# HGRN2 scores of levels 1 to 16 and the diagonal as 32x32 blocks in four 32-column tiles, masked copies of 96 columns, and the streams' state products in small tiles

## The chip, the core and the metric

The kernel runs on one core of one Trainium2 chip. The metric is the device time of one execution in microseconds, as the median of several runs: 1744.59 us for the kernel before, median of 3 runs between 1742.51 and 1745.06. The five engines that matter are TensorE (PE, with its weight loads as PEld), VectorE (DVE), ScalarE (ACT), GpSimd (POOL) and SyncE (SP), which issues the DMAs.

## The reference

One layer with two head groups: stick-breaking attention and an HGRN2 recurrence, whose outputs are gated, projected and normalised. Inputs are one new stream of 2048 frames and eight running streams of 16 frames each. The change touches the HGRN2 part alone, of 4 heads with key and value size 128:

```python
def hgrn2_recurrence(q, k, g, i, s0):
    """S_t = diag(f_t) S_{t-1} + k_t outer i_t,  o_t = S_t^T q_t,  g = log f, k = 1 - f."""
    ...
    def step(S, xs):
        qc, kc, gc, ic = xs
        b = jnp.cumsum(gc, axis=2)
        diff = b[:, :, :, None, :] - b[:, :, None, :, :]
        decay = jnp.where(causal, jnp.exp(jnp.minimum(diff, 0.0)), 0.0)
        scores = jnp.einsum('bhtd,bhsd,bhtsd->bhts', qc, kc, decay)
        o = (jnp.einsum('bhts,bhsv->bhtv', scores, ic)
             + jnp.einsum('bhtd,bhdv->bhtv', qc * jnp.exp(b), S))
        b_last = b[:, :, -1:, :]
        S_new = (jnp.exp(b_last)[:, :, 0, :, None] * S
                 + jnp.einsum('bhsd,bhsv->bhdv', kc * jnp.exp(b_last - b), ic))
        return S_new, o
```

So within a chunk each pair of a key time s and a query time t >= s has a score, which is a dot product over 128 channels with a decay of its own for each channel.

## The kernel before

The program has two halves. The first multiplies the frames by `w_in` (groups `pj`, L313 to L315 and L323 to L325: three products for each block of the contraction, of a high and a low part of each operand) and stores or keeps the sections of the result. In the same half the HGRN2 part runs, as 24 **chains**: 4 heads times 6 tiles of time. A tile is 384 columns, that is three chunks of 128 frames; the last of each half of the frames differs: once its third chunk holds the eight running streams (4 chains, `smp`), and once there are only two chunks (4 chains). The second half does the attention (L742 to L811), the streams' attention and the output projection, and does not change.

A chain is a generator, `hgrn` (L405). `weave` calls it between groups of six to twelve projection matmuls, one step at a time; two chains that are open take turns. The order on each engine is thus the order in which Python emits the instructions: a step of a chain stands between two groups of `pj` matmuls, and every engine runs its own queue in order. PE waits in its queue if the operands of a chain's step are late.

Scores come by **levels** m = 1, 2, 4, ... 64. Time is halved again and again: at level m the pairs (s, t) count whose times lie in the two halves of one block of 2m frames. Before the product, `q` of the later half and `kS` (the keys, 1 - f) of the earlier half have been scaled by the decay up to the border between the halves (L455, L456; `tot` holds the decay of whole blocks, L459). For m below 32, `scores` (L427) makes the full 128x128 product of each chunk in fp32, into one PSUM tile `ps`, and a masked copy (`copy_predicated`, L447, 128x384) takes from it the pairs of this level into `sc`; the masks are `lev`. For m = 32 and 64 only the blocks that count are made (L443), in PSUM partitions that start at 0 or 64, and are copied (L450). A matmul in fp32 shows as two records in the trace, for its two passes.

The diagonal (s = t) goes another way: `dp` is the product of `q` and `kS` element by element (L423), split into a high part `dh` (ACT, L464) and a low part `dl` (POOL, L466), and a product with `ones` (L469, L470) sums it over the channels; a masked copy takes the diagonal (L471).

Then the keys are transposed (`pk`, `kN`), states are updated (`pu`, L486 to L497), and the output is `sc` times the values plus `q` times the states (`po`, L501 to L508). In an `smp` chain the third chunk has eight states `s0`, one for each stream. `qz` is `q` of the chunk spread over eight blocks of 128 columns, of which 16 are not zero (L479 to L481), and eight 128x128 products add up in one PSUM tile (L508). The new states come from two products of 512 columns (`pb`, L537) with `iz`, the values with all but one stream's rows zeroed (L532), followed by eight updates on DVE (L539).

PSUM tiles `ps` and `pb` come from a pool of two (`psc`). SBUF tiles of a chain (`hw`) have two buffers each.

Of the kernel before, what the change touches and what calls it, by code (L numbers as in the profile page):

```python
# [9 lines left out]
F32 = mybir.dt.float32  # L10
F32R = mybir.dt.float32r
U8 = mybir.dt.uint8
# [5 lines left out]
P = 128  # L18
# [30 lines left out]
def constants():  # L49
    i = np.arange(P)  # L50
    s, t = i[:, None], i[None, :]
    x = s ^ t
    lev = np.stack([(s < t) & (x >= m) & (x < 2 * m) for m in LEVELS[:NL]] + [s == t], 1)
    f = lambda a: np.ascontiguousarray(a, dtype=np.float32)
    c = {
        "ident": f(s == t),
        "ntri": f(np.where(t < s, 0.0, -2.0 ** 66)),
        "levels": f(lev),
        "tri16": f(np.arange(TS)[None, :] < (i % TS)[:, None]),
        "hmask": f((i // TS)[:, None] == np.arange(H)[None, :]),  # L60
    }
    return c
# [3 lines left out]
def stream_step_kernel(ctx: ExitStack, tc: tile.TileContext, x_prompt, x_sample, cache_k, cache_v, state_s,  # L66
# [19 lines left out]
    lev = cst.tile([P, NL + 1, P], U8, name="lev")  # L86
    hmask = cst.tile([P, H], F32, name="hmask")
# [19 lines left out]
    def copy(eng, dst, src):  # L107
        if eng is act:
            act.copy(dst, src)  # L109
        elif eng is pool:  # L110
            pool.tensor_scalar(dst, src, 1.0, None, ALU.mult)
        else:
            eng.tensor_copy(dst, src)
# [84 lines left out]
    with ExitStack() as ph:  # L198
# [206 lines left out]
        def hgrn(half, h, hg, t0, nch):  # L405
# [13 lines left out]
            dp = hw.tile([P, TW], F32, name="dp", tag="kN")[:, :n]  # L419
            dh = hw.tile([P, TW], F32R, name="dh", tag="dh")[:, :n]  # L420
            dl = hw.tile([P, TW], F32R, name="dl", tag="dl")[:, :n]
            pool.memset(sc[:, :nch], 0.0)
            dve.tensor_tensor(dp, q, kS, ALU.mult)  # L423
            dve.tensor_tensor(q, q, f, ALU.mult)
            yield

            def scores(k):  # L427
                ps = psc.tile([P, 4, P], F32, name="ps", tag="ps")
                for c in range(k):
                    mm(ps[:, c], ch(kS, c), ch(q, c), start=True, stop=True)  # L430
                return ps[:, :k]
# [3 lines left out]
            for li, m in enumerate(LEVELS):  # L435
                k = nch if m < TS else npr
                if m < BLK:
                    ps = scores(k)
                else:
                    ps = psc.tile([P, 4, P], F32, name="ps", tag="ps")  # L440
                    for s0_ in range(0, P, 2 * m):
                        for c in range(k):
                            mm(ps[s0_:s0_ + m, c, :m], kS[:, c * P + s0_:c * P + s0_ + m],  # L443
                               q[:, c * P + s0_ + m:c * P + s0_ + 2 * m], start=True, stop=True)
                def keep_scores():
                    if m < BLK:
                        dve.copy_predicated(sc[:, :k], lev[:, li:li + 1].to_broadcast([P, k, P]), ps)  # L447
                        return
                    for s0_ in range(0, P, 2 * m):
                        dve.tensor_copy(sc[s0_:s0_ + m, :k, s0_ + m:s0_ + 2 * m], ps[s0_:s0_ + m, :k, :m])  # L450
                nn = k * P
# [11 lines left out]
                if m == 2:  # L463
                    copy(act, dh, dp)  # L464
                if m == 4:
                    pool.tensor_tensor(dl, dp, f32(dh), ALU.subtract)  # L466
                yield
            ps = psc.tile([P, 4, P], F32, name="ps", tag="ps")[:, :nch]
            mm(ps, ones, dh, start=True, stop=False)  # L469
            mm(ps, ones, dl, start=False, stop=True)  # L470
            dve.copy_predicated(sc[:, :nch], lev[:, NL:NL + 1].to_broadcast([P, nch, P]), ps)  # L471
# [5 lines left out]
            if smp:  # L477
                qz = xr.tile([P, NB, P], F32, name="qz", tag="x")
                pool.memset(qz, 0.0)  # L479
                for b in range(NB):  # L480
                    pool.tensor_copy(qz[:, b, b * TS:(b + 1) * TS], ch(q, npr)[:, b * TS:(b + 1) * TS])  # L481
# [22 lines left out]
            if smp:  # L504
                c = npr
                mm(po[:, c], sc[:, c], iv(c), start=True, stop=False)
                for b in range(NB):
                    mm(po[:, c], qz[:, b], s0[:, b], start=False, stop=b == NB - 1)  # L508
# [20 lines left out]
            if smp:  # L529
                yield  # L530
                iz = qz
                pool.tensor_tensor(iz, iv(npr).unsqueeze(1).to_broadcast([P, NB, P]), bc(hmask, P), ALU.mult)  # L532
                yield
                for b in range(NB):
                    if b % 4 == 0:
                        pb = psc.tile([P, 4, P], F32, name="pb", tag="ps")
                        mm(pb, kN[:, npr], iz[:, b:b + 4], start=True, stop=True)  # L537
                    o = npr * P // TS + b
                    dve.scalar_tensor_tensor(s0[:, b], s0[:, b], tot16[:, o:o + 1], pb[:, b % 4], ALU.mult, ALU.add)  # L539
                defer(lambda: dma.dma_start(s_sample[0, :, h].rearrange("b d e -> d b e"), s0), 2)  # L540


        def small():
            levf = xr.tile([P, NB, P], F32, name="levf", tag="x")[:, :NL + 1]
# [757 lines left out]
```

## Time and profile before

The profiled execution took 1747.05 us, with a span of 1745.2 us from its first to its last instruction.

| engine | busy us | share of the span | instructions |
|---|---|---|---|
| PE | 1672.4 | 96% | 12901 |
| PEld (weight loads) | 1519.8 | 87% | 12901 |
| DVE | 971.0 | 56% | 1762 |
| ACT | 710.9 | 41% | 1641 |
| POOL | 776.6 | 44% | 870 |

A matmul's record begins when it starts to read its moving operand and ends when the modelled result is there, so records of consecutive matmuls overlap, and the cost of one in a stream is the distance from its start to the next one's start. Views of the trace that are used: the page (shares of engines, the span in 40 slices), the table of stages (busy time of each engine in a stretch of the span), the groups by line and shape (count, busy time, mean duration of one, idle time before and who ended it), the waits (who waited for whom), and the timeline, in which neighbours of one line and shape are merged: start, length from the first start to the last end, and count.

### The profile page before, as it was taken

How to read it: one execution, taken by the hardware profiler on the slowest of the kernel's cores; microseconds unless marked ns; L12 is line 12 of the kernel's file. 1: busy time of each engine (PE TensorE's matmuls, PEld its weight loads, DVE VectorE, ACT ScalarE, POOL GpSimd, SP SyncE). 2: the span in 40 equal slices, each digit the busy share in tenths (PEclk: the TensorE clock that was granted, in tenths of full speed). 3: DMA queues.
4: the chain of work that ended last, by engine and by line, in shares of the span. 5: the costliest groups of instructions: out<-in, count | busy, mean ns of one | idle time of the engine just before them, and what ended most of it. 6: DMA issues, size and time to landing. Idle time of an engine off the chain costs nothing.

```text
span 1745.2 us, 33561 instructions
## 1 busy us (share of the span) xinstructions
PE 1672.4 (96%) x12901; PEld 1519.8 (87%) x12901; DVE 971.0 (56%) x1762; ACT 710.9 (41%) x1641; POOL 776.6 (44%) x870
## 2 busy tenths in 40 slices
PE   8999999999989999999999978999999999999998
PEld 8999999999989999999999966877887777778886
DVE  4264444255634263641647337787887686665554
ACT  3231221221323132221223246777877897775110
POOL 1242313232341142221323346777777776665664
PEclk9999999999999999999999989999999999999999
DMA  4233132122345133231212388899795754431443
GB/s 156 62 108 105 61 98 81 41 72 67 94 129 166 37 110 87 67 111 43 73 51 90 111 208 168 195 206 237 166 222 123 216 160 113 100 89 60 133 146 115
DMA packets 298790, 204.12 MB, mean 117 GB/s; under 512 B 113532, under 2 KB 275848, under 8 KB 298632
## 3 DMA queue, kind: packets, MB, share of 16 engines
q1 hardware_dynamic: 298632, 201.98, 43.5%
q8 instruction: 103, 1.69, 0.4%
q14 instruction: 55, 0.45, 0.1%
HBM read 146.36 MB, written 56.10 MB: 116 GB/s over the span
## 4 chain that ended last, share of the span: by engine, by line
PE 81%; DVE 5%; ACT 4%; DMA 4%; issue 2%; POOL 2%; SPq 1%; POOLq 0%; DVEq 0%; ACTq 0%
PE pj L313 10%; PE pj L315 10%; PE pj L314 10%; PE po L795 6%; PE z L742 5%; PE wt L777 5%; PE ps L430 4%; PE pj L323 4%; PE pj L325 4%; PE pj L324 4%; PE py L1132 3%; PE py L1134 3%; PE py L1133 3%; PE pk L877 2%; DVE kS L456 2%
## 5 line engine op out<-in xcount | busy, mean ns | idle before, releaser
L313 PE MATMUL pj<-xh,wh 128*128 128x384 f32 (+1 forms) x1152 | 395.7, 343 | 0.0
L764 POOL TENSOR_TENSOR s<-s,pr 128x512 f32<-128x512 f32 (+3 forms) x320 | 324.1, 1019 | 120.0 <-DVE pr L711 97.9
L315 PE MATMUL pj<-xh,wl 128*128 128x384 f32 (+1 forms) x1152 | 376.2, 327 | 0.0
L314 PE MATMUL pj<-xl,wh 128*128 128x384 f32 (+1 forms) x1152 | 375.7, 326 | 0.0
L117 POOL TENSOR_TENSOR wl<-wr,wh 128x512 fp32r<-128x512 f32 x126 | 164.2, 1327 | 387.9 <-ACT wh L109 387.9
L711 DVE TENSOR_TENSOR_SCAN pr<-keep,pr,one 128x513 f32<-128x513 f32 x192 | 238.6, 1270 | 46.7 <-ACT keep L750 35.0
L313 PEld LDWEIGHTS pj<-xh,wh 128*128 128x128 f32 x1152 | 217.4, 189 | 3.0 <-issue 1.0
L314 PEld LDWEIGHTS pj<-xl,wh 128*128 128x128 f32 x1152 | 217.5, 189 | 0.7 <-issue 0.7
L315 PEld LDWEIGHTS pj<-xh,wl 128*128 128x128 f32 x1152 | 216.7, 188 | 0.0
L742 PE MATMUL z<-kst,qr 128*128 128x512 f32 (+3 forms) x640 | 187.6, 404 | 17.9 <-ACT keep L750 6.3
L109 ACT COPY wh<-wt 128x512 f32<-128x512 f32 (+3 forms) x320 | 165.9, 550 | 78.4 <-PE wt L777 76.7
L747 ACT ACTIVATE s<-z 128x512 f32<-128x512 f32 (+3 forms) x320 | 184.6, 577 | 16.3 <-PE z L744 9.7
L777 PE MATMUL wt<-ident,s 128*128 128x128 f32 x1088 | 165.0, 279 | 2.1 <-POOL s L764 1.9
L323 PE MATMUL pj<-wh,xh 128*128 128x256 f32 x544 | 161.2, 296 | 0.0
L324 PE MATMUL pj<-wl,xh 128*128 128x256 f32 x544 | 153.0, 281 | 0.8 <-POOL wl L117 0.8
L777 PEld LDWEIGHTS wt<-ident,s 128*128 128x128 f32 x1088 | 123.2, 142 | 34.9 <-issue 16.4
L325 PE MATMUL pj<-wh,xl 128*128 128x256 f32 x544 | 152.8, 281 | 0.0
L117 POOL TENSOR_TENSOR e<-ev,e 128x384 fp32r<-128x384 f32 (+1 forms) x48 | 45.3, 943 | 221.1 <-ACT e L109 152.4
L795 PEld LDWEIGHTS po<-wh,vst 128*64 128x64 f32 x2176 | 119.1, 138 | 26.4 <-issue 16.2
L742 PEld LDWEIGHTS z<-kst,qr 128*128 128x128 f32 x640 | 106.0, 197 | 39.7 <-ACT keep L750 19.9
L795 PE MATMUL po<-wh,vst 128*64 128x128 f32 x2176 | 138.5, 279 | 0.0
L750 ACT ACTIVATE keep<-z 128x512 f32<-128x512 f32 (+2 forms) x230 | 134.6, 585 | 0.0
(164 smaller groups left out, 2907.0 us busy)
## 6 DMA issues: line engine op xcount, KB each, us to landing
wr<-in_w_in SPq DMA_DIRECT2D x64, 512.0 KB
qr<-qT_d SPq DMA_DIRECT2D x64, 256.0 KB
kr<-in_cache_k SPq DMA_DIRECT2D x16, 1024.0 KB
vr<-in_cache_v SPq DMA_DIRECT2D x32, 512.0 KB
kst<-kT_d SPq DMA_DIRECT2D x24, 512.0 KB
mt<-mx_d SPq DMA_DIRECT2D x136, 64.0 KB
x<-in_x_prompt SPq DMA_DIRECT2D x16, 512.0 KB
out<-xr SPq DMA_DIRECT2D x16, 512.0 KB
```

What stands on the lines that cost most here:

```text
L117: eng_lo.tensor_tensor(lo, src, f32(hi), ALU.subtract)
L313: mm(o, wh[:, k], xh[:, k, :n], start=k == 0, stop=False)
L314: mm(o, wh[:, k], xl[:, k, :n], start=False, stop=False)
L315: mm(o, wl[:, k], xh[:, k, :n], start=False, stop=k == KT - 1)
L323: mm(o, xh[:, k, ts], wh[:, k], start=k == 0, stop=False)
L324: mm(o, xh[:, k, ts], wl[:, k], start=False, stop=False)
L325: mm(o, xl[:, k, ts], wh[:, k], start=False, stop=k == KT - 1)
L711: dve.tensor_tensor_scan(pr[:, CW - wd:CW + 1][:, ::-1], kr, by, carry, ALU.mult, ALU.bypass)
L742: mm(z[:, :wd], q[:, a, r, q0:q0 + P], k[:, a, k0:k0 + wd], start=r == 0, stop=r == 1 and not top)
L764: pool.tensor_tensor(s[:, :wd], s[:, :wd], pr[:, CW - wd + 1:CW + 1], ALU.mult)
L777: nc.tensor.transpose(pt_[:, x:x + P], U[(u, a)][0][:, x:x + P], ident)
L795: mm(o[r], v[:, lo // P % 8 + x, r], th[a][:, x * P:(x + 1) * P], start=top and x == 0, stop=bot and x == n - 1, skip_group_check=True)
```

## The change

1. The masks `lev` shrink from 128 to 32 columns for each level: column j of row s now stands for the time that lies j into the 32-block of s.
2. For m below 32, `near` makes four 32x32 products per chunk instead of one 128x128 product: those of the 32-blocks on the diagonal of the chunk. Block number i of a chunk is written to PSUM partitions 32i to 32i+31, which are the array's column tile i; the four follow each other, chunk by chunk.
3. The masked copies (`keep`) have 96 columns (three chunks of 32), into a new tile `sd`, which POOL clears. At level 32, four copies on POOL bring `sd` into the diagonal blocks of `sc`.
4. The diagonal (s = t) is made by `near` too, of `q0`, the unscaled `q`, into other columns of the PSUM bank that level 1 uses; `dp`, `dh`, `dl` and the products with `ones` are gone. So that `q0` stays, the scaled `q` has a tile of its own, `qf`.
5. At levels 32 and 64 the loops are swapped: chunk by chunk, and the column tiles within.
6. In `smp` chains, `qz` has 32 columns for each stream instead of 128. The eight products go into 32 output partitions each, that is into the column tile that holds the two streams of 16 frames; streams 0, 2, 4, 6 first and then 1, 3, 5, 7. `iz` has four blocks instead of eight; the two `pb` products contract over 64 partitions each (0 to 63 and 64 to 127) and follow each other before the eight DVE updates.

```diff
@@ -49,15 +49,16 @@
 def constants():
     i = np.arange(P)
     s, t = i[:, None], i[None, :]
-    x = s ^ t
-    lev = np.stack([(s < t) & (x >= m) & (x < 2 * m) for m in LEVELS[:NL]] + [s == t], 1)
+    u = s // BLK * BLK + np.arange(BLK)[None, :]
+    x = s ^ u
+    lev = np.stack([(s < u) & (x >= m) & (x < 2 * m) for m in LEVELS[:NL]] + [s == u], 1)
     f = lambda a: np.ascontiguousarray(a, dtype=np.float32)
     c = {
 ...
         "levels": f(lev),
         "tri16": f(np.arange(TS)[None, :] < (i % TS)[:, None]),
-        "hmask": f((i // TS)[:, None] == np.arange(H)[None, :]),
+        "hmask": f((i // TS % 4)[:, None] == np.arange(4)[None, :]),
     }
     return c
 
@@ -83,8 +84,8 @@
     ntri = cst.tile([P, P], F32R, name="ntri")
     ones = cst.tile([P, P], F32R, name="ones")
     pool.memset(f32(ones), 1.0)
-    lev = cst.tile([P, NL + 1, P], U8, name="lev")
-    hmask = cst.tile([P, H], F32, name="hmask")
+    lev = cst.tile([P, NL + 1, BLK], U8, name="lev")
+    hmask = cst.tile([P, 4], F32, name="hmask")
 
     qT_d = scr.tile([4, 2, P, T], F32, name="qT_d")
     kT_d = scr.tile([4, 2, P, T], F32, name="kT_d")
@@ -416,38 +417,49 @@
             kS = hw.tile([P, TW], F32, name="kS", tag="kS")[:, :n]
             dve.tensor_scalar(kS, f, -1.0, 1.0, ALU.mult, ALU.add)
             sc = hw.tile([P, 3, P], F32, name="sc", tag="sc")
-            dp = hw.tile([P, TW], F32, name="dp", tag="kN")[:, :n]
-            dh = hw.tile([P, TW], F32R, name="dh", tag="dh")[:, :n]
-            dl = hw.tile([P, TW], F32R, name="dl", tag="dl")[:, :n]
+            sd = hw.tile([P, 3, BLK], F32, name="sd", tag="sd")
+            q0, q = q, hw.tile([P, TW], F32, name="qf", tag="qf")[:, :n]
             pool.memset(sc[:, :nch], 0.0)
-            dve.tensor_tensor(dp, q, kS, ALU.mult)
-            dve.tensor_tensor(q, q, f, ALU.mult)
-            yield
-
-            def scores(k):
-                ps = psc.tile([P, 4, P], F32, name="ps", tag="ps")
+            pool.memset(sd[:, :nch], 0.0)
+            dve.tensor_tensor(q, q0, f, ALU.mult)
+            yield
+
+            def near(ps, q, k):
                 for c in range(k):
-                    mm(ps[:, c], ch(kS, c), ch(q, c), start=True, stop=True)
-                return ps[:, :k]
+                    for s0_ in range(0, P, BLK):
+                        r = slice(c * P + s0_, c * P + s0_ + BLK)
+                        mm(ps[s0_:s0_ + BLK, c], kS[:, r], q[:, r], start=True, stop=True)
+
+            def keep(ps, li, k):
+                dve.copy_predicated(sd[:, :k], lev[:, li:li + 1].to_broadcast([P, k, BLK]), ps[:, :k])
 
             tot = f
             tot16 = None
             for li, m in enumerate(LEVELS):
                 k = nch if m < TS else npr
+                bank = psc.tile([P, 4, P], F32, name="ps", tag="ps")
+                ps = bank[:, :, :BLK]
                 if m < BLK:
-                    ps = scores(k)
+                    if li == 0:
+                        p0 = bank[:, :, BLK:2 * BLK]
+                        near(p0, q0, nch)
+                    near(ps, q, k)
                 else:
-                    ps = psc.tile([P, 4, P], F32, name="ps", tag="ps")
-                    for s0_ in range(0, P, 2 * m):
-                        for c in range(k):
+                    ps = bank
+                    for c in range(k):
+                        for s0_ in range(0, P, 2 * m):
                             mm(ps[s0_:s0_ + m, c, :m], kS[:, c * P + s0_:c * P + s0_ + m],
                                q[:, c * P + s0_ + m:c * P + s0_ + 2 * m], start=True, stop=True)
+
                 def keep_scores():
                     if m < BLK:
-                        dve.copy_predicated(sc[:, :k], lev[:, li:li + 1].to_broadcast([P, k, P]), ps)
+                        if li == 0:
+                            keep(p0, NL, nch)
+                        keep(ps, li, k)
                         return
                     for s0_ in range(0, P, 2 * m):
                         dve.tensor_copy(sc[s0_:s0_ + m, :k, s0_ + m:s0_ + 2 * m], ps[s0_:s0_ + m, :k, :m])
+
                 nn = k * P
                 q4 = q[:, :nn].rearrange("p (b two m) -> p b two m", two=2, m=m)
                 k4 = kS[:, :nn].rearrange("p (b two m) -> p b two m", two=2, m=m)
@@ -460,15 +472,11 @@
                 tot = nt
                 if m == 8:
                     tot16 = nt
-                if m == 2:
-                    copy(act, dh, dp)
-                if m == 4:
-                    pool.tensor_tensor(dl, dp, f32(dh), ALU.subtract)
+                if m == BLK:
+                    for s0_ in range(0, P, BLK):
+                        r = slice(s0_, s0_ + BLK)
+                        pool.tensor_copy(sc[r, :nch, r], sd[r, :nch])
                 yield
-            ps = psc.tile([P, 4, P], F32, name="ps", tag="ps")[:, :nch]
-            mm(ps, ones, dh, start=True, stop=False)
-            mm(ps, ones, dl, start=False, stop=True)
-            dve.copy_predicated(sc[:, :nch], lev[:, NL:NL + 1].to_broadcast([P, nch, P]), ps)
             pk = pt.tile([P, 4, P], F32, name="pk", tag="pt")
             for c in range(nch):
                 nc.tensor.transpose(pk[:, c], ch(kS, c), ident)
@@ -476,9 +484,10 @@
             act.copy(kN[:, :nch], pk[:, :nch])
             if smp:
                 qz = xr.tile([P, NB, P], F32, name="qz", tag="x")
-                pool.memset(qz, 0.0)
-                for b in range(NB):
-                    pool.tensor_copy(qz[:, b, b * TS:(b + 1) * TS], ch(q, npr)[:, b * TS:(b + 1) * TS])
+                pool.memset(qz[:, :, :2 * TS], 0.0)
+                for a in range(2):
+                    pool.tensor_copy(qz[:, a::2, a * TS:(a + 1) * TS],
+                                     ch(q, npr).rearrange("p (b a t) -> p b a t", a=2, t=TS)[:, :, a])
             yield
             po = pho.tile([P, 4, P], F32, name="po", tag="po")
             pu = pt.tile([P, 4, P], F32, name="pu", tag="pt")
@@ -503,9 +512,10 @@
                     mm(po[:, c], ch(q, c), olds[c], start=False, stop=True)
             if smp:
                 c = npr
-                mm(po[:, c], sc[:, c], iv(c), start=True, stop=False)
-                for b in range(NB):
-                    mm(po[:, c], qz[:, b], s0[:, b], start=False, stop=b == NB - 1)
+                mm(po[:, c], sc[:, c], iv(c), start=True, stop=True)
+                for b in [*range(0, NB, 2), *range(1, NB, 2)]:
+                    r = slice(b // 2 * 2 * TS, (b // 2 + 1) * 2 * TS)
+                    mm(po[r, c], qz[:, b, :2 * TS], s0[:, b], start=False, stop=True, skip_group_check=True)
             ms = hw.tile([P, 4], F32, name="ms", tag="ms")
             mo = hw.tile([P, 3, P], F32, name="mo", tag="mo")
             for c in range(nch):
@@ -528,20 +538,23 @@
                 dma.dma_start(s_prompt[0, 0, h], st[h][(c0 // 3 + 3 * half + 1) % 3])
             if smp:
                 yield
-                iz = qz
-                pool.tensor_tensor(iz, iv(npr).unsqueeze(1).to_broadcast([P, NB, P]), bc(hmask, P), ALU.mult)
+                iz = qz[:, :4]
+                pool.tensor_tensor(iz, iv(npr).unsqueeze(1).to_broadcast([P, 4, P]), bc(hmask, P), ALU.mult)
                 yield
+                pbs = []
+                for b in range(2):
+                    pbs.append(psc.tile([P, 4, P], F32, name="pb", tag="ps"))
+                    r = slice(b * DH, (b + 1) * DH)
+                    mm(pbs[b], kN[r, npr], iz[r], start=True, stop=True)
                 for b in range(NB):
-                    if b % 4 == 0:
-                        pb = psc.tile([P, 4, P], F32, name="pb", tag="ps")
-                        mm(pb, kN[:, npr], iz[:, b:b + 4], start=True, stop=True)
+                    pb = pbs[b // 4]
                     o = npr * P // TS + b
                     dve.scalar_tensor_tensor(s0[:, b], s0[:, b], tot16[:, o:o + 1], pb[:, b % 4], ALU.mult, ALU.add)
                 defer(lambda: dma.dma_start(s_sample[0, :, h].rearrange("b d e -> d b e"), s0), 2)
 
 
         def small():
-            levf = xr.tile([P, NB, P], F32, name="levf", tag="x")[:, :NL + 1]
+            levf = xr.tile([P, NL + 1, BLK], F32, name="levf", tag="x")
             dma.dma_start(levf, levels_d)
             dma.dma_start(hmask, hmask_d)
             vraw = xr.tile([12, P], F32, name="vraw", tag="x")
```

Three places in the order of instructions. First PE at the start of a chain's scores. Before, three 128x128 products `ps` stand between two groups of the projection:

```order
L315 MATMUL pj<-xh,wl 128x384
L430 MATMUL ps<-hq,kS 128x128 x3
L313 MATMUL pj<-xh,wh 128x384
L314 MATMUL pj<-xl,wh 128x384
L315 MATMUL pj<-xh,wl 128x384
```

With the change the same place holds twelve products of the unscaled `q` (named `hq`) for the diagonal and twelve of level 1 (named `qf`); the next levels have twelve each:

```order
L316 MATMUL pj<-xh,wl 128x384
L431 MATMUL ps<-hq,kS 32x32 x12
L431 MATMUL ps<-qf,kS 32x32 x12
L314 MATMUL pj<-xh,wh 128x384
L315 MATMUL pj<-xl,wh 128x384
L316 MATMUL pj<-xh,wl 128x384
```

The products have become smaller and four times as many, and those of the diagonal have moved from the chain's end to its first step; the projection around them is unchanged.

Second PE at the output of an `smp` chain, where `st` and `stt` are the states of the new stream and `s` those of the running streams. Before:

```order
L501 MATMUL po<-hi,sc 128x128
L503 MATMUL po<-stt,hq 128x128
L506 MATMUL po<-hi,sc 128x128
L508 MATMUL po<-s_1482,qz 128x128 x8
L313 MATMUL pj<-xh,wh 128x384
```

and with the change:

```order
L510 MATMUL po<-hi,sc 128x128
L512 MATMUL po<-stt,qf 128x128
L515 MATMUL po<-hi,sc 128x128
L518 MATMUL po<-s_1592,qz 32x128 x8
L314 MATMUL pj<-xh,wh 128x384
```

The eight products keep their place and write 32 partitions each.

Third POOL in the first `smp` chain, where `wl` is the low part of the projection's weights and `rs` belongs to the norm of the output. Before:

```order
L117 TENSOR_TENSOR wl<-wr,wh 128x512 x2
L422 MEMSET sc 128x384
L466 TENSOR_TENSOR dl<-dp,dh 128x384
L479 MEMSET qz 128x1024
L481 COPY qz<-hq 128x16 x8
L131 TENSOR_SCALAR rs<-ms 128x3
L132 TENSOR_TENSOR rs<-rs,nhalf 128x3
L117 TENSOR_TENSOR wl<-wr,wh 128x512 x2
L532 TENSOR_TENSOR qz<-hi,hmask 128x1024
```

and with the change:

```order
L118 TENSOR_TENSOR wl<-wr,wh 128x512 x2
L422 MEMSET sc 128x384
L423 MEMSET sd 128x96
L478 COPY sc<-sd 32x3x32 x4
L487 MEMSET qz 128x8x32
L489 COPY qz<-qf 128x4x16 x2
L132 TENSOR_SCALAR rs<-ms 128x3
L133 TENSOR_TENSOR rs<-rs,nhalf 128x3
L118 TENSOR_TENSOR wl<-wr,wh 128x512 x2
L542 TENSOR_TENSOR qz<-hi,hmask 128x512
```

The subtraction for `dl` is gone and four copies have come in, three levels later; the clearing of `qz` covers a quarter of the columns, its eight copies have become two, and the product with `hmask` is half as wide.

## The prediction

> **What bounds the kernel now.** I read the table of stages first, then the waits of PE, then the timeline of PE around a chain's step. The stages (length, then busy time with instruction count of PE, PEld, DVE, ACT, POOL, the granted clock, DMA):
>
> ```profile
> 0.00:60.00 60.00, 53.63 (x373) 51.93 (x374) 22.75 (x49) 18.96 (x32) 10.12 (x15) 1.00 0.44 141
> 60.00:1008.00 948.00, 927.42 (x6626) 902.18 (x6624) 437.04 (x1094) 222.18 (x567) 273.13 (x308) 1.00 0.29 85
> 1008.00:1100.00 92.00, 74.01 (x589) 60.44 (x591) 56.94 (x69) 59.32 (x137) 55.56 (x78) 0.87 0.80 177
> 1100.00:1745.00 645.00, 617.33 (x5319) 505.28 (x5315) 454.25 (x550) 410.44 (x907) 437.78 (x470) 0.99 0.61 153
> ```
>
> From 60 to 1008 us, where projection and chains run, PE is busy 927 of 948 us at full clock, DVE 437, POOL 273, and the DMA engines at 0.29. So PE alone bounds this half, and a microsecond taken from PE's queue there is a microsecond of the kernel. The second half has no instruction of the change; I take it as shifted as a whole. What PE waits for in the first half (total, times, longest):
>
> ```profile
> PE ps L430 <- DVE kS L456: 8.4, 9, 1.4
> PE pq L522 <- DVE on L518: 2.6, 3, 1.3
> PE ps L430 <- DVE sc L447: 2.6, 2, 1.3
> PE pb L537 <- POOL qz L532: 2.5, 1, 2.5
> ...
> PE ps L469 <- DVE sc L450: 1.1, 2, 0.7
> PE ps L430 <- DVE tot L459: 1.1, 4, 0.3
> ```
>
> Some 18 us, of which 15.8 us for DVE's work in the chains: small, but not nothing.
>
> **What one block of scores costs PE now.** The timeline of PE (start, length to the last end, line, count):
>
> ```profile
> 85.96 0.34 PE L315 MATMUL pj<-xh,wl 128*128 128x384 f32 x1
> 86.14 0.83 PE L430 MATMUL ps<-hq,kS 128*128 128x128 f32 x6
> 86.72 0.42 PE L313 MATMUL pj<-xh,wh 128*128 128x384 f32 x1
> 86.98 0.34 PE L314 MATMUL pj<-xl,wh 128*128 128x384 f32 x1
> 87.16 0.34 PE L315 MATMUL pj<-xh,wl 128*128 128x384 f32 x1
> 87.33 0.33 PE L313 MATMUL pj<-xh,wh 128*128 128x384 f32 x1
> ```
>
> A projection matmul follows the other by 0.175 us (86.98 to 87.33 is two). From 85.96 to 86.98 are 1.02 us; less two such steps the block of three chunks costs 0.67 us, that is 0.111 us for each of its six records. Two chunks cost 0.45.
>
> **What a block of 32x32 products costs.** Level 32 does them already, in two column tiles, six products (12 records) one tile after the other:
>
> ```profile
> 940.18 0.34 PE L315 MATMUL pj<-xh,wl 128*128 128x384 f32 x1
> 940.44 0.47 PE L443 MATMUL ps<-hq,kS 128*32 128x32 f32 x12
> 940.84 0.44 PE L313 MATMUL pj<-xh,wh 128*128 128x384 f32 x1
> 941.12 0.34 PE L314 MATMUL pj<-xl,wh 128*128 128x384 f32 x1
> 978.66 0.33 PE L443 MATMUL ps<-hq,kS 128*32 128x32 f32 x8
> ```
>
> 940.18 to 941.12, less 0.35, is 0.59 us. A record here takes 0.20 us by itself (L443 below), so first to last start is 0.27 us and **0.32 us are lost to entering and leaving the small tiles**: the first starts 0.26 us after a projection matmul, and the projection's second start comes 0.28 us after its first. That price is paid once per block, whatever is in it. How fast four tiles run together is seen in the streams' attention of the second half, with records of 128 columns:
>
> ```profile
> 1102.04 0.43 PE L958 MATMUL so<-vs,swN 128*32 128x128 f32 x8
> 1102.28 1.93 PE L958 MATMUL so<-vr,swT 128*32 128x128 f32 x64
> 1102.03:1102.07 0.04, 0.03 (x4) 0.03 (x5) 1.00 0.71 154
> ```
>
> 64 records from first to last start take 1.93 - 0.27 = 1.66 us, 26 ns each: four tiles carry 128 columns every 0.105 us, each as fast as the whole array above. The last row counts four starts within 40 ns. For 32 columns one tile needs a quarter of 0.111, 28 ns, at least; the row x8 (four records in each of two tiles, 0.13 us from first to last start) allows 43 at most. I take 32, near the lower end, since the x8 row holds the slow first weight load. Three chunks give each tile six records: 0.05 + 4 x 0.032 + 0.02 for the stagger of the tiles = **0.20 us**, and the block 0.52. Two chunks give 0.14, the doubled blocks of level 1 0.40 (three chunks) and 0.27 (two).
>
> **The sum on PE.** Counts and prices by these groups (count | busy, mean ns | idle before):
>
> ```profile
> L430 PE MATMUL ps<-hq,kS 128*128 128x128 f32 x672 | 95.4, 276 | 12.0 <-DVE kS L456 8.4 <-DVE sc L447 2.6 <-DVE tot L459 1.1
> L443 PE MATMUL ps<-hq,kS 128*32 128x32 f32 x256 | 10.0, 200 | 0.2 <-DVE kS L456 0.2
> L447 DVE COPY_PREDICATED sc<-lev,ps 128x384 f32<-128x384 uint8 x96 | 56.3, 586 | 0.0
> L447 DVE COPY_PREDICATED sc<-lev,ps 128x256 f32<-128x256 uint8 x24 | 10.6, 443 | 0.0
> L469 PE MATMUL ps<-dh,ones 128*128 128x384 f32 x20 | 7.1, 354 | 1.1 <-DVE sc L450 1.1
> L469 PE MATMUL ps<-dh,ones 128*128 128x256 f32 x4 | 1.2, 303 | 0.0
> L537 PE MATMUL pb<-qz,kN 128*128 128x512 f32 x16 | 9.1, 700 | 2.5 <-POOL qz L532 2.5
> ```
>
> The masked copies count the blocks: 96 of three chunks and 24 of two; 20 and 4 of them are level 1.
> - Levels 2 to 16: 76 blocks x (0.52 - 0.67) = -11.4; 20 of two chunks x (0.46 - 0.45) = +0.2.
> - Level 1, with the diagonal's products: 20 x (0.72 - 0.67) = +1.0; 4 x (0.59 - 0.45) = +0.6.
> - Products with `ones` gone: 20 x 2 x 0.175 = -7.0; 4 x 2 x 0.12 (two thirds of it) = -1.0.
> - Level 32 in turns: 16 blocks of three chunks, 0.27 to 0.19 = -1.3; two chunks and level 64 unchanged.
> - Output of the running streams, now:
>
> ```profile
> 160.08 1.95 PE L508 MATMUL po<-s,qz 128*128 128x128 f32 x16
> ```
>
>   16 records at 0.111 = 1.78 us; then four rounds of four tiles at 0.11, plus 0.32 = 0.76. Four chains: -4.1.
> - New states: four records of 512 columns, each 0.43 (between 4 x 0.105 and 4 x 0.111), 1.71 us a chain. No row shows two tiles of 64 rows at once. Ends: one after the other, with the switch, 2.03 (+1.3 in all), or together, 0.86 + 0.32 = 1.18 (-2.1). I take together, since column tiles do run so (L958).
>
> Together **-25 us**.
>
> **What goes beside PE.** DVE: from 586 and 443 ns for 384 and 256 columns, 1.1 ns a column, a copy of 96 is an estimated 0.26 us; 120 of them save 0.3 each, the diagonal's product and copy another 1 us a chain. This is worth something only where PE waits for DVE: a level's three DVE operations shorten from 1.7 us (0.51 + 0.61 + 0.59, L455, L456, L447) by a fifth:
>
> ```profile
> L455 DVE TENSOR_TENSOR hq<-hq,tot 128x192 f32<-128x192 f32 x108 | 55.0, 509 | 36.7 <-PE ps L430 26.0 <-PE ps L443 10.2
> L456 DVE TENSOR_TENSOR kS<-kS,tot 128x192 f32<-128x192 f32 x108 | 65.7, 608 | 0.0
> L466 POOL TENSOR_TENSOR dl<-dp,dh 128x384 fp32r<-128x384 f32 x20 | 21.1, 1072 | 6.8 <-ACT dh L109 6.8
> L481 POOL COPY qz<-hq 128x16 f32<-128x16 f32 x32 | 4.7, 198 | 4.1 <-DVE hq L455 3.9
> L532 POOL TENSOR_TENSOR qz<-hi,hmask 128x1024 f32<-128x1024 f32 x4 | 7.6, 1899 | 0.0
> L117 POOL TENSOR_TENSOR wl<-wr,wh 128x512 fp32r<-128x512 f32 x126 | 164.2, 1327 | 387.9 <-ACT wh L109 387.9
> ```
>
> Bounds for those waits: none of 15.8 goes, or all; as PE's shorter blocks also leave DVE less time, I take a quarter, **-4**, and -1 of the 2.5 us for `qz`, whose product halves. POOL: `dl` goes (1.07 us a chain), four copies of 32x96 come, at 0.2 (a 128x16 copy) to 0.4 us: no net load. The first waits for DVE's last masked copy, and behind it in POOL's queue stand `wl` for the next section and the stores' low parts; POOL idles 388 us before `wl`, waiting for ACT, which is the cover. Without it each `wl` that is late would cost PE up to 1.3 us. The copies themselves are needed by `po` three steps later, several us. The new DVE wait, for the clearing of `sd`, stands right behind that for `sc`.
>
> **Total:** -25 - 5 = -30 us. The profiled execution took 1747.05 us and would take 1717; the median of the runs stands 2.5 us below it, so the forecast is **1715 us**.
>
> **The rivals.**
> 1. *Small records don't come that fast (slower).* L443's twelve records stand 0.27/11 = 24.5 ns apart on the mean. In a block of 24 the mean distance p has to be paid 23 times; over all blocks (76 x 23 + 20 x 15 + 20 x 47 + 4 x 31 = 3112 distances) the sum without waits is 3112 p - 52 us (my p, 0.20/23 = 8.7 ns, gives the -25 back). It turns at p = 16.8 ns. With 24.5 it is +24: **1769**. For it: no row shows more than a dozen such short records. Against it: x8 has 0.13/7 = 18.5 ns with two tiles, so tiles overlap, and four of them start within 40 ns in L958. Chance 0.11. The Trainium skill's "TensorE: Matmul & The Clock Gate", section "Wait — 56ns, not 53.3ns?", states that the distance of starts never falls below about 25 ns, however few columns; by that rule the sum would be an estimated +26 us, 1771. The count of four starts in 40 ns disagrees with it across tiles, though nothing here shows it for long.
> 2. *Queueing in between.* A near block has 48 loads and matmuls within 0.2 us, level 1 96; if they are supplied only every 13 ns a record, the sum is 3112 x 0.013 - 52 = -12: **1733**. The same comes if PE, faster now, waits for `kS` twice as long (+16 against -25 gives 1736). Chance 0.18.
> 3. *More goes:* all 18 us of waits with the 25: **1702**. Chance 0.09.
> 4. *Both halves of rival 2 together*, or a later start of the attention's loads (DMA 0.80 behind 1008 us): no change, 1741 to 1748. Chance 0.07.
>
> **How the numbers follow.** Forecast (1705 to 1726) 0.55. The range 1702 to 1742 takes it in with rival 2 and the near part of rival 3, and leaves out about 0.2. The measurement tells 0.2% (3.5 us) from no change; faster than that: 0.55 + 0.18 + 0.09 = 0.82; within 0.07; slower 0.11.
>
> **What would show it.** In the changed kernel's timeline, a block of levels 2 to 8 (x24) should last 0.20 + 0.20 = 0.40 us and cost 0.52 between the projection's starts; over 0.55 us of length means rival 1. The x48 block of level 1 tells whether supply lags: 0.60 is right, over 0.8 is rival 2. PE's waits for L456 should be under 8 us in total. The first attention product now starts here:
>
> ```profile
> 1009.70 0.43 PE L742 MATMUL z<-kst,qr 128*128 128x128 f32 x2 [1.96 <-issue]
> ```
>
> It should start near 980, and from there to the end both kernels should take equally long; if not, the second half isn't simply shifted and the forecast is wrong there.

## The result, and the profile after

The changed kernel takes **1714.26 us** (median of 4 runs, 1713.33 to 1714.75) against 1744.82 us for the kernel before in the same comparison: a ratio of 0.9827, with a 95% interval from 0.9809 to 0.9844. The forecast was 1715 us.

The table of stages of the changed kernel, cut at the same places of the program (length, busy time with count of PE, PEld, DVE, ACT, POOL, granted clock, DMA):

```profile
0.00:60.00 60.00, 54.09 (x383) 52.72 (x384) 22.77 (x49) 18.94 (x32) 9.65 (x15) 1.00 0.44 136
60.00:976.00 916.00, 901.09 (x9119) 848.48 (x9118) 362.25 (x1070) 211.74 (x542) 268.79 (x376) 1.00 0.30 88
976.00:1066.00 90.00, 72.88 (x575) 59.97 (x575) 54.80 (x68) 56.79 (x131) 52.91 (x79) 0.87 0.84 183
1066.00:1712.00 646.00, 618.76 (x5342) 506.95 (x5340) 455.70 (x552) 413.03 (x913) 439.93 (x473) 0.99 0.61 153
```

Nearly all of the gain lies in the first half, now 976 instead of 1008 us; PE is as full as before (901 of 916 us), and DVE lost 75 us of work. The second half is the old one, shifted: the first attention product starts here,

```profile
978.08 0.41 PE L755 MATMUL z<-kst,qr 128*128 128x128 f32 x2 [0.77 <-issue]
```

at 978.1 instead of 1009.7, and from there to the end it is 734.2 us (span 1712.3) instead of 735.5, so 1.3 us of the difference lie behind the change. The timeline of PE at the start of a chain, the doubled block of level 1 and two of the blocks behind it:

```profile
84.11 0.34 PE L316 MATMUL pj<-xh,wl 128*128 128x384 f32 x1
84.38 0.39 PE L431 MATMUL ps<-hq,kS 128*32 128x32 f32 x24
84.59 0.42 PE L431 MATMUL ps<-qf,kS 128*32 128x32 f32 x24
84.94 0.44 PE L314 MATMUL pj<-xh,wh 128*128 128x384 f32 x1
85.22 0.34 PE L315 MATMUL pj<-xl,wh 128*128 128x384 f32 x1
...
88.24 0.34 PE L316 MATMUL pj<-xh,wl 128*128 128x384 f32 x1
88.51 0.40 PE L431 MATMUL ps<-qf,kS 128*32 128x32 f32 x24
88.84 0.45 PE L314 MATMUL pj<-xh,wh 128*128 128x384 f32 x1
89.12 0.34 PE L315 MATMUL pj<-xl,wh 128*128 128x384 f32 x1
```

A block of 24 records lasts 0.40 us, that is 0.20 from first to last start, and costs 0.53 (88.24 to 89.12, less 0.35) where the three 128x128 products cost 0.67. The double block costs 0.76 (84.11 to 85.22, less 0.35).

To see where the 30 us come from, I added up PE's time in the first half by kind of step: from the start of the projection matmul before a step to the start of the second one behind it, less their own 0.175 us (0.12 for 256 columns). By this reckoning the first half's last projection matmul starts 30.4 us sooner, made up of:

| part | before, us | after, us | difference | forecast |
|---|---|---|---|---|
| scores of levels 1 to 16 (120 steps; after: with the diagonal) | 94.3 | 81.3 | -13.0 | -9.6, and -4 of waits |
| steps with `ones` and the keys' transposes | 17.9 | 9.1 | -8.8 | -8.0 |
| level 32 | 14.7 | 13.3 | -1.4 | -1.3 |
| output of `smp` chains | 11.6 | 7.6 | -4.1 | -4.1 |
| new states of the streams | 11.2 | 6.8 | -4.4 | -2.1, and -1 of waits |
| transposes of the input | 16.2 | 14.5 | -1.7 | none |
| all else, the projection's own steps among it | | | +3.0 | none |

The transposes at the start wait for the first loads and differ between executions: 14.5 to 17.9 us among the kernels below, which all do the same there.

About 2 of the 3 us of "all else" are the granted clock. In the first half it falls to half for 3.4 us at a time, once in the kernel before and twice in the changed one (rows as in the table of stages; the clock is the third number from the right):

```profile
521.80:525.30 3.50, 3.09 (x5) 1.51 (x5) 0.98 (x4) 0.00 (x0) 0.35 (x1) 0.51 0.44 157
```

```profile
504.80:508.20 3.40, 3.40 (x13) 3.40 (x12) 1.81 (x8) 0.00 (x0) 0.00 (x0) 0.50 0.31 100
747.10:750.60 3.50, 3.50 (x43) 3.15 (x44) 1.19 (x7) 0.00 (x0) 0.00 (x0) 0.51 0.99 280
```

Before, the stretch lies on one step of the streams' new states; after, both lie mostly on the projection's own matmuls. Each begins during a wait of PE or at most 1.5 us behind one (of 2.5, 1.7 and 0.9 us). But a wait of 1.7 us at the same place is followed by none in experiments 1 and 5, so what decides is not shown.

### The profile page after: what moved, and what is told of

Same layout as the page of the kernel before. It is cut to its first block, busy times and chain, and to the rows that moved or that the text cites. A ratio compares the mean times of both kernels' runs of the same rounds, so it can differ in the third digit from the quotient of the medians.

```text
span 1712.3 us, 38577 instructions
## 1 busy us (share of the span) xinstructions
PE 1646.8 (96%) x15413; PEld 1468.1 (86%) x15413; DVE 895.5 (52%) x1738; ACT 700.5 (41%) x1617; POOL 771.3 (45%) x942
## 4 chain that ended last, share of the span: by engine, by line
PE 85%; ACT 5%; DMA 3%; DVE 3%; POOL 1%; issue 1%; SPq 0%; POOLq 0%; DVEq 0%; ACTq 0%
PE pj L314 12%; PE pj L316 10%; PE pj L315 10%; PE po L808 7%; PE z L755 6%; PE wt L790 6%; PE pj L324 4%; PE py L1145 4%; PE pj L326 4%; PE pj L325 4%; PE py L1147 4%; PE py L1146 4%; PE ps L431 2%; PE pk L890 2%; ACT keep L763 1%
```

## The experiments

**1. Do the tiles have to take turns?** The four column tiles one after the other instead of chunk by chunk:

```diff
-                for c in range(k):
-                    for s0_ in range(0, P, BLK):
+                for s0_ in range(0, P, BLK):
+                    for c in range(k):
```

> The changed kernel, with the 32x32 products of a block issued tile after tile (all chunks of column tile 0, then all of tile 1, ...) instead of chunk by chunk with the four tiles in turn. Same work, same copies. Theory (four tiles stream side by side only as long as the queue brings each of them its next record; before, in L443, the second tile of six records began about 0.09 us after the first): a block of 24 records lasts 3 x 0.09 + 0.18 = 0.45 us from first to last start instead of 0.20, level 1 about 0.9 instead of 0.44, blocks of two chunks stay; 76 x 0.25 + 20 x 0.45 = +28 us, 1742 us. Rival A (the array sorts the tiles out by itself, order does not matter): 1714 us, block 0.20. Rival B (one tile after the other with no overlap, 28 ns a record): block 0.64 us, +55 us, 1769 us.

1736.96 us, ratio 0.9963 (0.9949 to 0.9977) to the kernel before. The timeline of PE of this kernel:

```profile
89.30 0.34 PE L316 MATMUL pj<-xh,wl 128*128 128x384 f32 x1
89.57 0.65 PE L431 MATMUL ps<-qf,kS 128*32 128x32 f32 x24
90.14 0.44 PE L314 MATMUL pj<-xh,wh 128*128 128x384 f32 x1
90.42 0.34 PE L315 MATMUL pj<-xl,wh 128*128 128x384 f32 x1
```

The block lasts 0.65 us, 0.45 from first to last start, as the theory has it, and the doubled block 0.81 from first to last start. So most of the gain hangs on the order of the loops: with the tiles in sequence a block costs 0.77 us (89.30 to 90.42, less 0.35), more than the big products did. The time is 5 us below the 1742 of the theory. The array does not sort it out by itself; nor does it run the tiles with no overlap.

**2. What does the diagonal cost now?** Its products and its copy are left out:

> The changed kernel with the diagonal (s = t) left out of the scores: no products of q0, no masked copy of them. It measures what the diagonal costs in its new form. Theory: the block of level 1 falls from 48 to 24 records and from a cost of 0.76 to 0.53 us (three chunks) and from 0.59 to 0.46 (two): 20 x 0.23 + 4 x 0.13 = -5 us against the changed kernel, 1709 us; so of the 8.8 us that the products with ones gave back, 5 were spent again. Rival (the second 24 records ride nearly free in a block that is open anyway): -2 us or less.

1709.36 us in a single run. The projection ends 4.2 us sooner than in the changed kernel, although the transposes of the input took 3.4 us longer in this execution. The doubled blocks have become plain ones. So the way through `ones` cost 8.8 us, and the new way spends 5 of them again: without the diagonal the steps of levels 1 to 16 take 76.1 us instead of 81.3.

**3. The streams' products alone**, on the kernel before (the edits to `qz`, the eight products, `iz` and `pb`, nothing else):

> The kernel before with only the streams' part of the change: qz in 32 columns, eight products into 32 partitions each, iz of four blocks, two pb products of 64 partitions. Scores and diagonal as before. Theory: 4 chains x (1.0 us at po, and 1.1 us at pb, of which half is the wait for qz) = -8.5 us against the kernel before, 1736 us, ratio 0.995. Rival (these blocks hide behind DVE and POOL work of the same chain, whose waits take the place): no change, ratio within 0.001 of 1.

1735.76 us, ratio 0.9953 (0.994 to 0.9967). As expected: the streams' part stands for itself and adds up with the rest. In the changed kernel its eight products read:

```profile
155.13 0.65 PE L518 MATMUL po<-s,qz 128*32 128x128 f32 x16
```

0.65 us instead of 1.95, with the switch to be added.

**4. Sharing the switch.** Where two chains are open, both step at every second place, so that two small-tile blocks stand together:

```diff
             credit[0] = min(credit[0] + rate, 2.0)
+            if credit[0] < min(len(chains), 2):
+                return
             while credit[0] >= 1.0 and step_chain():
```

> The changed kernel with another weave: where two chains are open, both make their step at every second place instead of one at each, so that two blocks of 32x32 products stand together on PE. Same work. Theory (about 0.33 us are lost to each entering and leaving of the small tiles, whatever the block holds): some 50 pairs share it, -16 us; a block of 48 records lasts 0.04 longer than two of 24, +2, and DVE has two chains' steps to do within the same stretch, some waits more: 1704 us, and at most 1710. Rival (the price is not per entering but per record, or PE then waits for DVE for as long as it saves): 1714 us or more, with PE's waits for L468 over 20 us in total.

1727.34 us, ratio 0.9912 (0.9898 to 0.9925): a miss, 13 us slower than the changed kernel. The price is as assumed: an undisturbed double block costs 0.76 us against 2 x 0.53. But PE waits (this kernel, total, times, longest):

```profile
PE ps L431 <- DVE sd L434: 11.9, 8, 2.8
PE pq L532 <- DVE on L528: 8.7, 11, 1.3
PE ps L451 <- DVE sc L461: 7.9, 6, 2.2
PE ps L431 <- DVE kS L468: 7.3, 8, 1.0
```

35.8 us in these four rows, where the changed kernel has 12.1. The first stands at 2.3 us there: a score block needs one of two PSUM tiles, and the masked copy that frees it stands on DVE behind the decay products. The clock falls to half in five stretches of the first half instead of two, which adds to the loss.

**5. Are DVE's shorter copies worth anything?** Every masked copy is made twice:

```diff
-                dve.copy_predicated(sd[:, :k], ...)
+                for _ in range(2):
+                    dve.copy_predicated(sd[:, :k], ...)
```

> The changed kernel with each masked copy of 96 columns made twice, so that DVE spends about as long on them per level as before the change (2 x 0.26 us against 0.59). PE's work is the same. Theory (some 5 of the 13 us that the levels gained came from DVE's shorter copies, since a chain's step takes DVE 1.7 us and more of the 2.1 us that PE gives it): +4 to +8 us against the changed kernel, 1718 to 1722 us, and PE's waits for DVE in the levels, now 12 us, at 16 or more. Rival (DVE has room, the shorter copies are worth nothing): 1714 us.

1716.31 us (ratio 0.9839, 0.981 to 0.9869, against 0.9827, 0.9809 to 0.9844). The projection ends at 977.1 us, as in the changed kernel (977.0), but that is a balance: this execution had no stretch at half the clock, and its transposes of the input took 1.4 us longer. The steps of levels 1 to 16 tell it better: 82.0 us instead of 81.3. PE's waits there, in the changed kernel and in this one, only change their name:

```profile
PE ps L431 <- DVE kS L468: 7.2, 8, 1.0
PE ps L431 <- DVE sd L434: 2.3, 2, 1.1
```

```profile
PE ps L431 <- DVE sd L435: 6.6, 8, 1.0
PE ps L431 <- DVE kS L469: 4.1, 4, 1.2
```

They are 9.5 and 10.7 us in total, where 16 or more were expected. The rival is right: the shorter copies are worth about 1 us to PE at most. My forecast of 4 us for them had the wrong cause.

**6. Is it the bank?** In the doubled block, the last dozen records start 10.6 ns apart on the mean, many of them in twos some 16 ns apart, where the first two dozen come every 8.7 (0.43 us from first to last start, where 0.40 were forecast).

```diff
-                        p0 = bank[:, :, BLK:2 * BLK]
+                        p0 = pt.tile([P, 4, P], F32, name="p0", tag="pt")[:, :, :BLK]
```

> The changed kernel with the diagonal's products in a PSUM bank of their own (from the pool of the transposes) instead of other columns of level 1's bank. In the doubled block of level 1 the first 34 records or so come every 8 ns, the others every 16. Theory (the queue does not bring more short records than that at such a pace): nothing changes, the block of 48 still lasts 0.43 us from first to last start, 1714 us. Rival (two groups in one bank disturb each other): 0.39 us or less, -1 us.

The expectation misreads the trace where it has 16 ns for every record behind the 34th. 1714.12 us in a single run, and 19 of 20 doubled blocks still 0.43 us (one 0.53): not the bank. Why the last dozen come late was not shown. Length alone does not set the pace: the eight blocks of 96 records in experiment 4 take 0.87 us on the mean, 9.2 ns a record, and there too it is the last dozen that come every 10.7 ns.

**7. and 8. No masked copies at all**, with pairs and without (the copies of levels 1 to 16 and of the diagonal left out):

> The kernel in which two chains make their steps in pairs, with the masked copies of levels 1 to 16 and of the diagonal left out, so that DVE has less to do. To be read against the next kernel, which leaves out the same in the changed kernel. Theory (sharing the entering and leaving does save 0.33 us a pair, and what took it away was waiting for DVE): 8 us or more below the next kernel. Rival (sharing saves nothing, or PE waits for something else): as the next kernel or above.

> The changed kernel with the masked copies of levels 1 to 16 and of the diagonal left out. Theory: some of the 12 us of PE's waits for DVE in the levels go, 1706 to 1711 us. Rival: DVE has room, 1714 us.

1712.15 us with pairs and 1716.04 us without, a single run each. The second confirms experiment 5: with no copies at all PE still waits as long (9.2 us instead of 9.5, and 81.0 us for the steps of levels 1 to 16). The first says that the pairs' loss is bound up with the copies, as the 11.9 us for `sd` are gone. But the pairs gain nothing then: the projection ends at 978.9 us with them and at 978.4 without. The 4 us between the two runs lie in the second half (731.5 and 735.8 us), which is the same in both, so they say nothing on pairs. In the levels the pairs do save 8 us, but 9.1 us of waits at the norm (`pq`) and 7.9 for `sc` stand against it, where the kernel without pairs has 2.6 and none worth counting.

**What does PE wait for, then?** I looked at each of PE's waits for a score block that was longer than 0.15 us (15 in the kernel before, 10 in the changed one). Every time, one of DVE's two decay products ran beside a two-operand operation on POOL, and took 0.7 to 1.4 us instead of 0.35. The timelines of DVE and of POOL in the changed kernel:

```profile
476.07 1.20 DVE L467 TENSOR_TENSOR qf<-qf,tot 128x192 f32<-128x192 f32 x1 [1.13 <-PE ps L431]
477.19 1.43 DVE L468 TENSOR_TENSOR kS<-kS,tot 128x192 f32<-128x192 f32 x1
...
479.22 0.36 DVE L467 TENSOR_TENSOR qf<-qf,tot 128x192 f32<-128x192 f32 x1 [0.33 <-PE ps L431]
479.50 0.35 DVE L468 TENSOR_TENSOR kS<-kS,tot 128x192 f32<-128x192 f32 x1
```

```profile
475.77 2.62 POOL L118 TENSOR_TENSOR wl<-wr,wh 128x512 fp32r<-128x512 f32 x2
```

The same products take 0.35 us when POOL has nothing to do, and each of the slow ones ends just behind one of the two `wl`. In the kernel before, `dl` stood beside such a product, or within about a microsecond ahead of it, at 13 of the 15 waits. The Trainium skill's "SBUF — State Buffer", section "SBUF: two separate sides", states that DVE, with two SBUF operands, and GpSimd hold a shared pair of ports in turn, each for a whole instruction. The trace agrees: the second product ends 0.23 us behind the pair of `wl` (478.62 and 478.39), as if it did its work only when POOL's operation was over, not at some shared rate. That gives two tests.

**9. `dl`'s place on POOL taken again**, by a subtraction that nobody reads:

```diff
+                if m == 4:
+                    dl = hw.tile([P, TW], F32, name="dl", tag="dl", bufs=1)[:, :n]
+                    pool.tensor_tensor(dl, q0, f, ALU.subtract)
```

> The changed kernel with one more POOL operation a chain: a subtraction of 128x384 at level 4, where the one for dl stood before; its result is read by nobody. PE's and DVE's work is the same. Theory (PE's waits for DVE in the levels fall on places where DVE's two decay products run beside a two-operand POOL operation and take 1.1 to 1.4 us instead of 0.35, and the change took 24 such POOL operations away): waits come back, +2 to +5 us against the changed kernel, 1716 to 1719, and PE's waits for DVE in the levels at 13 us or more instead of 10 to 12. Rival (only wl on POOL does that, or the waits are chance): 1714 us.

1716.56 us, ratio 0.9848 (0.983 to 0.9866) where the changed kernel has 0.9827: in time alone the intervals overlap. In the profile the projection ends at 982.1 us, 5.1 later. Of that, 3.1 us lie in the steps of levels 1 to 16 (84.4 us instead of 81.3); the rest lies at the start, in the transposes of the input and the first projection matmuls. The two main rows have 12.3 us of waits, just under the 13 that were expected:

```profile
PE ps L431 <- DVE kS L468: 9.1, 9, 1.7
PE ps L431 <- DVE sd L434: 3.2, 4, 1.1
```

(7.2 and 2.3 in the changed kernel). The theory holds: `dl`'s place costs about 3 us, clear of the 0.5 us by which the same steps differ between the changed kernel and experiment 6 (81.3 and 80.8), and in one profiled execution each. That is 3 of the 5 us which the levels gained beyond the prices of undisturbed blocks, not all of them.

**10. `wl` on DVE:**

```diff
-                    split(act, dve if i == 0 and e else pool, hi[:, ks], lo[:, ks], r[:, kr])
+                    split(act, dve, hi[:, ks], lo[:, ks], r[:, kr])
```

> The changed kernel with the low parts of the projection's weights (wl, 126 subtractions of 128x512) on DVE instead of POOL; the rest as it is. Theory (beside wl on POOL DVE's decay products take four times as long; wl on DVE costs DVE about 0.7 us each, 88 us in all, with DVE at 40% in this half): nine of the ten waits of about 1 us go, but wl stands ahead of some chain steps on DVE: -3 us, 1711, within 1705 to 1716; decay products of 1.1 us and more nearly gone. Rival (DVE's queue becomes the wait instead): over 1716 us.

**1707.89 us**, ratio 0.9807 (0.9788 to 0.9827): the fastest kernel here, though its interval overlaps that of the changed kernel. The groups of DVE in the changed kernel and in this one (count | busy, mean ns | idle before):

```profile
L468 DVE TENSOR_TENSOR kS<-kS,tot 128x192 f32<-128x192 f32 x108 | 58.9, 545 | 0.0
```

```profile
L468 DVE TENSOR_TENSOR kS<-kS,tot 128x192 f32<-128x192 f32 x108 | 38.2, 353 | 0.0
L118 DVE TENSOR_TENSOR wl<-wr,wh 128x512 fp32r<-128x512 f32 x128 | 88.2, 733 | 33.5 <-ACT wh L110 27.1 <-DMA out<-kn 6.1
```

The decay product is at its 0.35 us throughout, `wl` takes DVE 0.73 us each where POOL needed 1.33, and PE's waits for `kS` fall from 7.2 to 2.3 us. The steps of levels 1 to 16 take 72.9 us instead of 81.3, but the norm's transposes take 14.0 instead of 11.1; the projection ends at 970.8 us instead of 977.0. Two waits of 1.2 us remain where two `wl` stand in DVE's queue ahead of a step.

**11. Pairs and `wl` on DVE together:**

> Both together: steps of two open chains in pairs, and wl on DVE. Theory (sharing saves about 14 us on PE, and what took it away was DVE slowed down by POOL in the longer stretch of two steps): below 1710 us, 1702 at best. Rival (DVE is simply too busy with two steps and now wl too): 1715 us or more.

1712.0 us in a single run, between theory and rival and no better than `wl` on DVE alone. By the reckoning of the first section, the steps of levels 1 to 16 take PE 60 us instead of 73, or 10 us less when the keys' transposes that now stand alone are counted in, so shared switches do pay now; the 11.9 us of waits for `sd` in experiment 4 are down to 0.3, so those too came from `wl` on POOL. The projection ends 1.9 us later all the same (972.7 us). The norm's transposes (`pq`) take 21 instead of 14, probably because with pairs the projection between two steps no longer hides the way from POOL over DVE to them; levels 32 and 64 take 2 us more, and three stretches at half the clock instead of one cost some 3:

```profile
PE pq L532 <- DVE on L528: 10.9, 13, 1.9
PE ps L451 <- DVE sc L461: 8.3, 7, 1.7
```

## Why the prediction was right, point by point

- **The bound** was right: the first half belongs to PE, what left PE's queue left the kernel, and the second half moved as a whole (734.2 and 735.5 us). Experiment 3 shows it for one part alone: 8.2 us, where the prediction's terms had 7.2 and the expectation 8.5.
- **A block of 32x32 products** was right: 0.20 us from first to last start and 0.32 for the switch were forecast; 0.20 and 0.33 are measured. The four tiles do carry 32 columns each in turn, 8.7 ns a record. Rival 1, with 24.5 ns, was the price of a bad order of issue, as level 32 (0.08 us less a block by the order alone) and experiment 1 show: L443's row came from two tiles one after the other, and its mean distance was no floor.
- **Level 1** was mis-sized by 0.04 us a block: 0.76 instead of 0.72, as the last dozen of 48 records come late, for a reason that stays open. With it, levels 1 to 16 gave 8.0 us by their undisturbed prices (76 x -0.14, 20 x +0.015, 20 x +0.09, 4 x +0.14), not 9.6. Rival 2 exists in this small form alone.
- **Products with `ones`**: -8.8 against -8.0, waits for the masked copy before them among it. **Level 32** and **the streams' output** came as forecast.
- **New states**: an undisturbed step went from 1.72 to 1.26 us, so the two tiles of 64 rows do run side by side, as was assumed without a row for it: -1.8 for four chains, where -2.1 was taken. The wait for `qz` gave 0.9, where -1 was forecast. The other 1.7 us of the -4.4 are the clock and were in no term: before, the four products behind that wait ran in the stretch at half the clock, 0.85 us each instead of 0.43; after, the two pairs of products did not.

```profile
522.21 3.48 PE L537 MATMUL pb<-qz,kN 128*128 128x512 f32 x4 [2.53 <-POOL qz L532]
```

```profile
503.30 1.13 PE L548 MATMUL pb<-qz,kN 64*128 64x512 f32 x4 [1.66 <-POOL qz L542]
```

- **Waits for DVE in the levels**: the size was right (-13.0 less -8.0 is -5, forecast -4), the cause was not. The step that failed is that DVE's shorter copies shorten PE's waits: doubling them cost these steps 0.7 us (experiment 5). The waits come from decay products beside POOL's two-operand operations, and the change took 24 of those away with `dl`; putting them back brought 3.1 us (experiment 9). About 1 us of the 5 is not placed. The prediction saw `dl` go and counted it as POOL's load only.
- **POOL's four copies** cost nothing that can be seen, as forecast.
- **The total** came within 1 us by luck as well: the transposes of the input (-1.7 us), the second half (-1.3) and all else (+3.0) stood at nothing in the sum and cancel, and a gain in waits of the forecast size had another cause.

## What to carry to other kernels

Products that use 32 of 128 columns pay as soon as four column tiles can take turns in the order of issue, and the fixed price of entering and leaving (0.33 us here) says how many must stand together: at 24 records the gain was 0.14 us of 0.67, at 16 there was none. Read where an engine waits by single instances, not by the group's mean: the mean of 0.55 us of a decay product hid a product of 0.35 and one of 1.4, and the second was POOL's doing. Before steps are packed together to save a switch, look for the chain that lived on the gap between them.

## What the runs showed of the hardware that was not expected

- Order of issue decides whether column tiles overlap: the same 24 records take 0.20 us with the tiles in turn and 0.45 tile after tile.
- In a block of 48 short records the last dozen come every 10.6 ns on the mean instead of every 8.7, in one PSUM bank or two; in a block of 96 it is again the last dozen (10.7).
- A DVE product of 0.35 us with two SBUF operands takes 1.1 to 1.4 us beside a POOL subtraction of 1.0 to 1.4 us.
- In a half where PE is busy at 98%, a wait of PE of 0.9 to 2.5 us was followed three times by 3.4 us at a granted clock of 0.50 (at 521.8 us before, at 504.8 and 747.1 after), and products of 512 columns then started 0.85 us apart instead of 0.43. What decides whether it follows is open.
